# A transposed feed-forward group taken whole: all wide products, then all narrow ones

## The chip, the cores and the metric

The kernel runs on one core of one Trainium2 chip. Time is device time in microseconds (us). The median of three runs before the change is 970.79 us (970.16 to 971.24).

The engines are TensorE (PE in the profile; PEld is its weight load), VectorE (DVE), ScalarE (ACT), GpSimd (POOL) and SyncE (SP), which here issues the transfers. Each works through its own queue in order. [...]

## The reference

Two decoder layers on 256 tokens of width 1024, in float32. Each layer has a feed-forward half step, a token mixer and a second feed-forward half step, each followed by a residual sum and a layer norm. So there are four feed-forward phases, and the change concerns only these:

```
def swiglu(x, w_gate, w_up, w_down):
    return (jax.nn.silu(x @ w_gate) * (x @ w_up)) @ w_down

x = layer_norm(ALPHA * x + 0.5 * swiglu(x, ffn1_gate[l], ffn1_up[l], ffn1_down[l]), ...)
```

The hidden width is 2816, the model width 1024.

## The kernel before

**Numbers.** A float32 matrix is split in two float32r parts: the high part (`xh`, `wh`, `dh`, `hth`) is a cast by ScalarE, the low part (`xl`, `wl`, `dl`, `htl`) a subtraction by VectorE (`halves`, L100 to L102). A product is made of three: high by high, high by low, low by high. `mm3` (L94 to L98) issues them one after the other, each of 512 columns.

**Tiling.** The hidden width is cut in 11 groups of 256 (`GW`). A group has four weight tiles of gate and up together (`gw[g]`, one for every two of the eight slices of 128 of the model width) and two of down (`dw[g]`). `G` makes gate and up of a group and `D(g, hf)` adds the group's down product for one half (128) of the tokens: twelve products, six into each of two banks.

**Turned groups.** Groups 2 to 9 (`turned`, L299) are computed transposed: the weights are the stationary operand (128 columns of the hidden width, a block `i` of two in a group), and the tokens move. Here the three products become two: a *wide* one, the high weights by high and low tokens side by side (512 columns, L314), and a *narrow* one, the low weights by the high tokens (256 columns, L312), which is added to the right half of the same bank. `G(g, n)` of a turned group makes block `n`: two banks, gate and up, and for each of the four weight tiles four wide and then four narrow products (`columns`, L302). Then `gate_turned` (L317) reads the banks: ScalarE copies the right half, VectorE adds the left half (L324, L325), and so for gate and for up; then silu, a product, and the split into `hth` and `htl`. The other groups (0, 1 and 10) have the tokens as the stationary operand; their result is transposed on TensorE by `T` (L396, L399), whose bank is then read by ScalarE and VectorE.

**Banks.** Eight: four called `acc` (`psa`), which hold the down sums, and four called `gu` (`psg`), which `G`, `T` and the transposes of the tokens take in turn, in a ring. Who writes a bank waits until its last content has been read.

**Weights.** They come in one fixed order (`stream`) through five staging tiles (`raw`), and are split into a ring of eight (`w`), of eight (`x`) or of six (`d`, down). `advance` loads on as far as rings are free; a tile's place is free after its last use (`used`, L145). ScalarE and VectorE take the splits and the read-outs from one queue each, in an order fixed when the program is built; `gate_turned`, `gate` and `T` ask for a higher priority than program order (`AHEAD`), weight splits for a lower one (`BEHIND`).

**Order on TensorE.** It is written out by hand in `run` (L431). In the loop over the turned groups, G(g, 0), D(g - 1, 0), G(g, 1), D(g - 1, 1) follow each other. `Later` keeps short pieces of work, such as `T`, that become due after so many ticks; a tick is three products of 512 columns (`mm3`) or as much (L315). `later.wait` issues due work early until a condition holds.

Of the kernel before, what the change touches and what calls it, by code (L numbers as in the profile page):

```python
# [10 lines left out]
F32 = mybir.dt.float32  # L11
# [6 lines left out]
P = 128  # L18
D = 1024
S = 256  # L20
DEPTH = 2
KT = D // P
DFF = 2816
GW = 256
# [50 lines left out]
def trunk(ctx: ExitStack, tc: tile.TileContext, t, out: bass.AP):  # L75
    nc = tc.nc
# [9 lines left out]
    psg = pool("psg", 4, space=PSUM)  # L86
    ctx.enter_context(tc.manual_schedule(engines={mybir.EngineType.PE}))
    later = Later()
# [80 lines left out]
    x, xT = [None, None], [None, None]  # L169
    xt2 = xtp.tile([P, KT, 2, 2, P], F32R, name="xt")  # L170
# [19 lines left out]
    def project(hf, ps, ws):  # L190

        xt = xT[hf]
        for kt in range(KT):
            later.wait(lambda: xt.done > kt)
            wh, wl = ws[kt // 2].parts
            cs = slice((kt % 2) * 512, (kt % 2) * 512 + 512)
            mm3(ps, xt.h[:, kt, :], xt.l[:, kt, :], wh[:, cs], wl[:, cs], kt == 0, kt == KT - 1)
            if kt % 2:
                ws[kt // 2].used()
# [66 lines left out]
    class FFN:  # L266
# [14 lines left out]
                for n in {0: [], 1: [0, 1], 2: [], NG - 1: [NG - 2, NG - 1]}.get(g, [g - 1]):  # L281
                    self.dw[n] = [Weight(dn[2 * n + i], "d", ND) for i in range(2)]

        def G(self, g, n):

            if self.turned(g):
                ps = [psg.tile([P, 2 * S], F32, name="gu") for _ in range(2)]
                for kq, w in enumerate(self.gw[g]):
                    later.wait(lambda: min(xT[0].done, xT[1].done) > 2 * kq + 1)
                    self.columns(kq, n, ps, w)  # L290
                    w.used()
                self.gate_turned(g, n, ps)
                return
            hf = n
            ps = psg.tile([P, 2 * GW], F32, name="gu")
            project(hf, ps, self.gw[g])
            self.gate(g, hf, ps)

        def turned(self, g):  # L299
            return 1 < g < NG - 1  # L300

        def columns(self, kq, i, ps, w):  # L302


            parts = [(kt, part) for kt in range(2) for part in range(2)]
            for lo in range(2):
                for kt, part in parts:
                    c = kt * 512 + part * GW + i * P
                    x = xt2[:, 2 * kq + kt].rearrange("p l h t -> p (l h t)")
                    first, last = kq + kt == 0, kq == KT // 2 - 1 and kt == 1  # L310
                    if lo:
                        nc.tensor.matmul(ps[part][:, S:2 * S], w.parts[1][:, c:c + P], x[:, 0:S], start=False, stop=last)  # L312
                    else:
                        nc.tensor.matmul(ps[part], w.parts[0][:, c:c + P], x, start=first, stop=False)  # L314
                later.tick()  # L315

        def gate_turned(self, g, i, ps):  # L317
            gate = scope[0].tile([P, S], F32, name="sil", bufs=2)
# [87 lines left out]
        def D(self, g, hf):  # L406
            if self.turned(g):
                ht = [[p[:, place[hf], :] for p in self.ht[g, i]] for i in range(2)]
            else:
                later.wait(lambda: (g, hf) in self.ht)  # L410
                ht = [[p[:, i, :] for p in self.ht[g, hf]] for i in range(2)]
            if g == 0:
                self.accs[hf] = [psa.tile([P, 512], F32, name="acc") for _ in range(2)]
            if g == 4 and hf == 0:
                self.gb = load_gb(*self.ln)
                if self.first:
                    load_consts()
                    for n in range(2):
                        load_x(n)
            dw = [w.parts for w in self.dw[g]]  # L420
            for c in range(2):
                cs = slice(c * 512, c * 512 + 512)
                for i in range(2):
                    mm3(self.accs[hf][c], ht[i][0], ht[i][1], dw[i][0][:, cs], dw[i][1][:, cs],
                        g == 0 and i == 0, g == NG - 1 and i == 1)
            for w in self.dw[g]:
                w.used()
            if g == NG - 1:
                layer_norm(hf, self.accs[hf], 0.5 / ALPHA, self.gb, self.slots[hf], self.last)

        def run(self):  # L431
            G, D = self.G, self.D
            if self.first:
                self.start()
                D(0, 0)
                D(0, 1)
                G(2, 0)
                D(1, 0)
                D(1, 1)
                G(2, 1)  # L440
            else:
                G(0, 0)
                G(1, 0)
                D(0, 0)
                G(0, 1)
                D(1, 0)
                G(1, 1)
                D(0, 1)
                G(2, 0)
                D(1, 1)  # L450
                G(2, 1)
            for g in range(3, NG - 1):
                G(g, 0)
                D(g - 1, 0)
                G(g, 1)
                if g < NG - 2:
                    D(g - 1, 1)
            G(NG - 1, 0)
            D(NG - 2, 0)
            D(NG - 1, 0)  # L460
            G(NG - 1, 1)
            if self.mixer_next:
                tc.keep_in_program_order(nc.scalar.preload_act_table_set("natural_log_exp_and_others"))
            if self.first:
                with tc.high_priority(offset=-BEHIND):
                    lower_bounds()
            for g in range(NG - 3, NG):
                D(g, 1)


    def lower_bounds():

        pr = rawp.tile([P, 2, 512], F32, name="raw")
        for i in range(2):
            late_dma(pr[:, i, :], t["lb"][i:i + 1, :].to_broadcast([P, 512]))
        p0, p1 = pr[:, 0, :], pr[:, 1, :]
        m, r = la, lm
        nc.vector.tensor_tensor(m, p0, p1, ALU.max)
        for p in (p0, p1):
            nc.vector.tensor_tensor(p, p, m, ALU.subtract)  # L480
            tc.keep_in_program_order(nc.scalar.activation(p, p, AF.Exp))
        nc.vector.tensor_tensor(m, p0, p1, ALU.add)
        for c in range(4):
            cs = slice(c * P, (c + 1) * P)
            nc.vector.reciprocal(r[:, cs], m[:, cs])
        for p in (p0, p1):
            nc.vector.tensor_tensor(p, p, r, ALU.mult)
        nc.vector.tensor_tensor(p1, p0, p1, ALU.add)
        nc.vector.tensor_tensor(p1, p1, p0, ALU.subtract)
        nc.vector.tensor_scalar(p0, p1, -1.0, 1.0, ALU.mult, ALU.add)  # L490
        for dst, v in ((m, p1), (r, p0)):
            nc.vector.tensor_scalar_max(dst, v, TINY)
            nc.scalar.activation(dst, dst, AF.Ln)
            nc.vector.tensor_scalar(v, v, 0.0, NEG, ALU.is_le, ALU.mult)
            nc.vector.tensor_tensor(dst, dst, v, ALU.add)
# [372 lines left out]
```

## Time and profile before

| | before |
|---|---|
| median of three runs | 970.79 us |
| profiled execution | 972.56 us |
| its span | 970.7 us |
| granted TensorE clock | 0.999 |
| busy: PE | 958.2 us (99%), 4814 products |
| busy: DVE | 677.4 us (70%) |
| busy: ACT | 525.6 us (54%) |
| DMA | 180.67 MB, mean 186 GB/s |

The span runs from the first to the last instruction of the profiled execution; the profiled execution took 1.86 us more than its span. A row of the page's groups has line, engine, operation, output<-inputs, shape and count, then busy time and mean duration, then the idle time ahead of it and what ended that. In a timeline a row has start, duration, engine, line, operation and count; neighbours of one line are merged, and [..] is the idle time before it and what ended it. Matmuls overlap, so the distance of their starts is their pace, not their duration. Names of tiles that share a buffer can stand for each other (`xh` for `wh`). The three later phases begin near 298, 485 and 776 us.

### The profile page before, as it was taken

What the parts mean: (1) busy time and instruction counts of PE and PEld (TensorE: products, weight loads), DVE (VectorE), ACT (ScalarE), POOL (GpSimd) and SP (SyncE); (2) the same over time, 40 slices, a digit from 0 to 9 for tenths busy, and PEclk for the clock granted to TensorE, in tenths of its full rate; (3) what the DMA queues carried; (4) which work ended last, traced back from release to release, by engine and by line L of the source; (5) the groups of instructions that cost most, each with busy time, mean ns of one, the idle gap of its engine ahead of it and who ended that gap; (6) DMA issues with size and microseconds to landing.
All of it is one profiled execution on the core that took longest, in us unless ns stands there. A gap on an engine that the chain in (4) does not pass through costs nothing.

```text
span 970.7 us, 13157 instructions
## 1 busy us (share of the span) xinstructions
PE 958.2 (99%) x4814; PEld 806.8 (83%) x4814; DVE 677.4 (70%) x1095; ACT 525.6 (54%) x810; POOL 26.2 (3%) x47
## 2 busy tenths in 40 slices
PE   9999999999999999999999999999999999999996
PEld 6888888788888888888788888888888888888885
DVE  5875765799779775665677666647897897665525
ACT  6765655367456664545436555533965466555420
POOL 0000000000010000000000000000001000000000
PEclk9999999999999999999999999999999999999999
DMA  8888654334436876555347755442334378755301
GB/s 283 327 299 301 227 209 161 109 109 132 151 111 229 309 243 217 196 195 173 104 162 251 262 186 208 166 139 97 131 130 168 101 275 286 239 199 208 109 1 44
DMA packets 51473, 180.67 MB, mean 186 GB/s; under 512 B 6096, under 2 KB 6352, under 8 KB 51408
## 3 DMA queue, kind: packets, MB, share of 16 engines
q1 hardware_dynamic: 51408, 179.83, 54.0%
q8 instruction: 38, 0.62, 0.3%
q14 instruction: 27, 0.22, 0.1%
HBM read 178.75 MB, written 1.05 MB: 185 GB/s over the span
## 4 chain that ended last, share of the span: by engine, by line
PE 95%; DMA 2%; DVE 1%; ACT 1%; issue 0%; SPq 0%; DVEq 0%
PE gu L314 23%; PE gu L312 12%; PE acc L97 10%; PE acc L95 10%; PE acc L96 10%; PE gu L97 8%; PE gu L95 8%; PE gu L96 8%; PE acc L650 2%; DMA raw<-in_dn 2%; PE gu L185 1%; PE acc L622 1%; PE acc L623 1%; DMA raw<-in_gu 1%; PE gu L399 1%
## 5 line engine op out<-in xcount | busy, mean ns | idle before, releaser
L102 DVE TENSOR_TENSOR wl<-raw,wh 128x1024 fp32r<-128x1024 f32 (+1 forms) x204 | 243.0, 1202 | 66.5 <-ACT wh L101 59.8
L101 ACT CAST wh<-raw 128x1024 fp32r<-128x1024 f32 (+1 forms) x204 | 210.3, 1035 | 97.1 <-PE gu L314 46.3
L314 PE MATMUL gu<-xt,wh 128*128 128x512 f32 x768 | 208.9, 393 | 0.0
L102 DVE TENSOR_TENSOR dl<-raw,dh 128x1024 fp32r<-128x1024 f32 x88 | 106.7, 1223 | 69.9 <-ACT dh L101 69.5
L314 PEld LDWEIGHTS gu<-xt,wh 128*128 128x128 f32 x768 | 134.6, 189 | 20.6
L95 PE MATMUL acc<-dh,hth 128*128 128x512 f32 x352 | 139.2, 395 | 1.8 <-ACT hth L101 1.8
L97 PE MATMUL acc<-dh,htl 128*128 128x512 f32 x352 | 138.7, 394 | 0.9 <-DVE htl L102 0.8
L96 PE MATMUL acc<-dl,hth 128*128 128x512 f32 x352 | 138.0, 392 | 0.0
L95 PE MATMUL gu<-wh,xt 128*128 128x512 f32 x336 | 135.1, 402 | 0.0
L97 PE MATMUL gu<-wh,xt 128*128 128x512 f32 x336 | 131.3, 391 | 0.0
L312 PEld LDWEIGHTS gu<-xt,wl 128*128 128x128 f32 x768 | 117.7, 189 | 16.0
L96 PE MATMUL gu<-wl,xt 128*128 128x512 f32 x336 | 130.9, 390 | 0.0
L101 ACT CAST dh<-raw 128x1024 fp32r<-128x1024 f32 x88 | 91.8, 1049 | 65.6 <-DMA raw<-in_dn 64.7
L312 PE MATMUL gu<-xt,wl 128*128 128x256 f32 x768 | 122.1, 281 | 0.0
L97 PEld LDWEIGHTS acc<-dh,htl 128*128 128x128 f32 x352 | 66.0, 188 | 16.8 <-DVE htl L102 2.9
L95 PEld LDWEIGHTS acc<-dh,hth 128*128 128x128 f32 x352 | 66.2, 188 | 14.6 <-ACT hth L101 3.2
L96 PEld LDWEIGHTS acc<-dl,hth 128*128 128x128 f32 x352 | 66.2, 188 | 11.9
L97 PEld LDWEIGHTS gu<-wh,xt 128*128 128x128 f32 x336 | 63.1, 188 | 13.6
L96 PEld LDWEIGHTS gu<-wl,xt 128*128 128x128 f32 x336 | 63.3, 188 | 12.1
L95 PEld LDWEIGHTS gu<-wh,xt 128*128 128x128 f32 x336 | 63.2, 188 | 12.0
L314 PE MATMUL gu<-xt,xh 128*128 128x512 f32 x256 | 70.3, 396 | 0.0
L324 ACT COPY sil<-gu 128x256 f32<-128x256 f32 x64 | 23.5, 368 | 68.8 <-PE gu L312 68.8
(156 smaller groups left out, 1049.3 us busy)
## 6 DMA issues: line engine op xcount, KB each, us to landing
raw<-in_gu SPq DMA_DIRECT2D x172, 512.0 KB, 4.5
raw<-in_dn SPq DMA_DIRECT2D x88, 512.0 KB, 4.9
raw<-in_win SPq DMA_DIRECT2D x40, 512.0 KB, 4.3
raw<-in_wout SPq DMA_DIRECT2D x16, 512.0 KB, 4.3
lng<-in_ln_g SPq DMA_DIRECT2D x6, 512.0 KB, 4.8
lnb<-in_ln_b SPq DMA_DIRECT2D x6, 512.0 KB, 5.9
raw<-in_gu SPq DMA_DIRECT2D x8, 256.0 KB, 6.7
raw<-in_cumM SPq DMA_DIRECT2D x2, 512.0 KB, 5.3
```

Of the source, the lines that this page charges most:

```text
L95: nc.tensor.matmul(ps, lh, wh, start=start, stop=False)
L96: nc.tensor.matmul(ps, lh, wl, start=False, stop=False)
L97: nc.tensor.matmul(ps, ll, wh, start=False, stop=stop)
L101: first = nc.scalar.copy(dst_h, src)
L102: return first, nc.vector.tensor_tensor(dst_l, src, dst_h.bitcast(F32), ALU.subtract)
L185: nc.tensor.transpose(pt[:, k - a, :], self.nat[:, k * P:(k + 1) * P], ident)
L312: nc.tensor.matmul(ps[part][:, S:2 * S], w.parts[1][:, c:c + P], x[:, 0:S], start=False, stop=last)
L314: nc.tensor.matmul(ps[part], w.parts[0][:, c:c + P], x, start=first, stop=False)
L324: nc.scalar.copy(dst, p[:, S:2 * S])
L399: nc.tensor.transpose(pt[:, i, :], hn[:, i * P:(i + 1) * P], ident)
L622: nc.tensor.matmul(pe, lh[:, hs], cumM[:, hf, cs], start=True, stop=False)
L650: nc.tensor.matmul(ps[B][0:rows, j, :], E[:, j, s0:s0 + rows], E[:, j, t0:t0 + ps[B].shape[2]], start=True, stop=True)
```

## The change

`G(g, 0)` and `G(g, 1)` of a turned group become one `GT(g)`. It takes all four `gu` banks, issues 32 wide products (per slice of the model width: gate and up of block 0, then of block 1), then the 16 narrow products of block 0, calls `gate_turned` for it, then the 16 of block 1, and `gate_turned` again. A weight tile is marked as used within the last 16 products. Ticks come every 3 x 512 columns. If the group before is not a turned one, `GT` first issues that group's transposes `T`, as far as they are still pending. In `run`, both D of the group before follow GT together (only the first for the last turned group, whose second follows at the end as before).

```diff
@@ -281,38 +281,43 @@
                 for n in {0: [], 1: [0, 1], 2: [], NG - 1: [NG - 2, NG - 1]}.get(g, [g - 1]):
                     self.dw[n] = [Weight(dn[2 * n + i], "d", ND) for i in range(2)]
 
-        def G(self, g, n):
-
-            if self.turned(g):
-                ps = [psg.tile([P, 2 * S], F32, name="gu") for _ in range(2)]
-                for kq, w in enumerate(self.gw[g]):
-                    later.wait(lambda: min(xT[0].done, xT[1].done) > 2 * kq + 1)
-                    self.columns(kq, n, ps, w)
-                    w.used()
-                self.gate_turned(g, n, ps)
-                return
-            hf = n
+        def G(self, g, hf):
             ps = psg.tile([P, 2 * GW], F32, name="gu")
             project(hf, ps, self.gw[g])
             self.gate(g, hf, ps)
 
+        def GT(self, g):
+            later.wait(lambda: self.turned(g - 1) or all((g - 1, hf) in self.ht for hf in range(2)))
+            ps = [[psg.tile([P, 2 * S], F32, name="gu") for _ in range(2)] for _ in range(2)]
+            n = 0
+            for lo in range(2):
+                w = S if lo else 2 * S
+                blocks = [[0], [1]] if lo else [[0, 1]]
+                for block in blocks:
+                    for kt in range(KT):
+                        later.wait(lambda: min(xT[0].done, xT[1].done) > kt)
+                        weight = self.gw[g][kt // 2]
+                        for i in block:
+                            for part in range(2):
+                                c = (kt % 2) * 512 + part * GW + i * P
+                                x = xt2[:, kt].rearrange("p l h t -> p (l h t)")
+                                nc.tensor.matmul(ps[i][part][:, 2 * S - w:], weight.parts[lo][:, c:c + P], x[:, 0:w],
+                                                 start=kt == 0 and not lo, stop=kt == KT - 1 and lo == 1)
+                                n += w
+                                if n >= 3 * 512:
+                                    n -= 3 * 512
+                                    later.tick()
+                        if kt % 2 and block == [1]:
+                            weight.uses = 1
+                            weight.used()
+                    if lo:
+                        self.gate_turned(g, block[0], ps[block[0]])
+
         def turned(self, g):
             return 1 < g < NG - 1
-
-        def columns(self, kq, i, ps, w):
-            parts = [(kt, part) for kt in range(2) for part in range(2)]
-            for lo in range(2):
-                for kt, part in parts:
-                    c = kt * 512 + part * GW + i * P
-                    x = xt2[:, 2 * kq + kt].rearrange("p l h t -> p (l h t)")
-                    first, last = kq + kt == 0, kq == KT // 2 - 1 and kt == 1
-                    if lo:
-                        nc.tensor.matmul(ps[part][:, S:2 * S], w.parts[1][:, c:c + P], x[:, 0:S], start=False, stop=last)
-                    else:
-                        nc.tensor.matmul(ps[part], w.parts[0][:, c:c + P], x, start=first, stop=False)
-                later.tick()
 
         def gate_turned(self, g, i, ps):
             gate = scope[0].tile([P, S], F32, name="sil", bufs=2)
@@ -429,15 +434,14 @@
                 layer_norm(hf, self.accs[hf], 0.5 / ALPHA, self.gb, self.slots[hf], self.last)
 
         def run(self):
-            G, D = self.G, self.D
+            G, GT, D = self.G, self.GT, self.D
             if self.first:
                 self.start()
                 D(0, 0)
                 D(0, 1)
-                G(2, 0)
+                GT(2)
                 D(1, 0)
                 D(1, 1)
-                G(2, 1)
             else:
                 G(0, 0)
                 G(1, 0)
@@ -446,13 +450,11 @@
                 D(1, 0)
                 G(1, 1)
                 D(0, 1)
-                G(2, 0)
+                GT(2)
                 D(1, 1)
-                G(2, 1)
             for g in range(3, NG - 1):
-                G(g, 0)
+                GT(g)
                 D(g - 1, 0)
-                G(g, 1)
                 if g < NG - 2:
                     D(g - 1, 1)
             G(NG - 1, 0)
```

## The prediction

> **What bounds the kernel now.** I read the page first (span, chain, costliest groups; L102 is the split of a weight's low half on VectorE, 1.2 us each).
>
> ```profile
> span 970.7 us, 13157 instructions
> PE 95%; DMA 2%; DVE 1%; ACT 1%; issue 0%; SPq 0%; DVEq 0%
> L102 DVE TENSOR_TENSOR wl<-raw,wh 128x1024 fp32r<-128x1024 f32 (+1 forms) x204 | 243.0, 1202 | 66.5 <-ACT wh L101 59.8
> L314 PE MATMUL gu<-xt,wh 128*128 128x512 f32 x768 | 208.9, 393 | 0.0
> ```
>
> TensorE sets the end: it is the chain for 95% of the span. The change removes no product, so it can gain in two ways only: the same products following each other closer, or a wait of TensorE going away. The durations (393 ns for a wide product) overlap and say nothing about pace; pace is read from starts. So next the timeline of TensorE at the end of a feed-forward phase (start, us, line, count): the 16 wide and 16 narrow products of G(9,1), then G(10,0) and D(9,0), which are wide throughout.
>
> ```profile
> 161.82 1.07 PE L314 MATMUL gu<-xt,wh 128*128 128x512 f32 x4
> 162.73 0.64 PE L312 MATMUL gu<-xt,wl 128*128 128x256 f32 x4
> 163.21 1.09 PE L314 MATMUL gu<-xt,wh 128*128 128x512 f32 x4
> 164.14 0.64 PE L312 MATMUL gu<-xt,wl 128*128 128x256 f32 x4
> 164.61 1.09 PE L314 MATMUL gu<-xt,xh 128*128 128x512 f32 x4
> 165.54 0.64 PE L312 MATMUL gu<-xt,xl 128*128 128x256 f32 x4
> 166.02 1.10 PE L314 MATMUL gu<-xt,xh 128*128 128x512 f32 x4
> 166.95 0.63 PE L312 MATMUL gu<-xt,xl 128*128 128x256 f32 x4
> 167.42 0.40 PE L95 MATMUL gu<-wh,xt 128*128 128x512 f32 x1
> ...
> 169.26 0.39 PE L97 MATMUL gu<-wh,xt 128*128 128x512 f32 x1
> ...
> 172.89 0.39 PE L95 MATMUL acc<-dh,hth 128*128 128x512 f32 x1
> ```
>
> G takes 167.42 - 161.82 = 5.60 us. Its four narrow runs take 0.48, 0.47, 0.48 and 0.47, so 0.119 per product. Its wide runs take 0.91 for the first, which follows wide products, and 0.93 for the others, which follow narrow ones. After the last narrow run the first eight wide products take 1.84 (0.230 each), the next sixteen 3.63 (0.2269 each). So wide products have a settled pace of 0.2269, and a switch from narrow to wide costs some of the following products a few ns each, until they settle.
>
> Is that price one of the switch, or a debt that each narrow product leaves? The mixer shows wide products behind a run of small ones (128 columns) that begins at 740.06:
>
> ```profile
> 740.06 0.60 PE L704 MATMUL gu<-ident,y 128*128 128x128 f32 x4
> ...
> 742.51 0.39 PE L96 MATMUL gu<-wl,xt 128*128 128x512 f32 x1
> ...
> 744.12 0.39 PE L97 MATMUL gu<-wh,xt 128*128 128x512 f32 x1
> ...
> 745.48 0.39 PE L97 MATMUL gu<-wh,xt 128*128 128x512 f32 x1
> ```
>
> Seven products in 1.61 (0.230 each), then six in 1.36 (0.2267 each): more than 2 us of small products leave what 0.47 us of narrow ones leave. It looks like a price of the switch. But the small ones are of another kind, so this is an argument by likeness.
>
> **The change part by part.**
>
> *Fewer switches, all 32 turned groups.* Before, a group has eight narrow-to-wide switches; after, one. Its 32 wide products start behind wide ones (D), so they run settled: 32 x 0.2269 = 7.26. For 32 narrow ones in a row no row exists. In the quads they take 0.1175 to 0.120; I take 0.1195, near the later ones of a run: 3.82. Together 11.08 against 2 x 5.60 = 11.20: 0.12 per group, 3.8 us over 32. For the bounds of the unknown narrow pace the nearest row is that of the wide ones, whose settled pace is 0.0056 from that in the quads (0.93/4 = 0.2325): taken with either sign for the narrow ones, it moves the sum by 32 x 32 x 0.0056 = 5.7 us both ways.
>
> *The two down products side by side.* The first D behind narrow products pays the switch; the second, now behind the first, does not.
>
> ```profile
> 67.11:69.88 2.77, 2.77 (x14) 2.25 (x13) 2.33 (x6) 1.91 (x4) 0.00 (x0) 1.00 0.77 280
> 172.89:175.62 2.73, 2.73 (x13) 2.21 (x12) 1.33 (x3) 0.39 (x1) 0.00 (x0) 1.00 0.00 0
> 349.11:352.42 3.31, 3.05 (x15) 2.18 (x14) 3.22 (x5) 1.93 (x5) 0.00 (x0) 1.00 0.57 194
> 536.57:539.70 3.13, 3.05 (x14) 2.18 (x13) 2.72 (x4) 1.66 (x4) 0.00 (x0) 1.00 0.58 219
> 827.44:831.25 3.81, 3.25 (x15) 2.10 (x13) 3.34 (x5) 2.54 (x6) 0.00 (x0) 1.00 0.37 130
> ```
>
> These are stretches by engine (length first): a D behind narrow products 2.77, behind wide ones 2.73. Six pairs in each of four phases (groups 3 to 8) become neighbours: 24 x 0.04 = 1.0 us.
>
> *A stall that loses its place.* The last three rows are D(2,0) of the second, third and fourth phase: 0.54, 0.36 and 1.04 over 2.77, 1.9 us together. It waits for the low half of group 2's second block, made on VectorE behind the split of down weights that are just landing:
>
> ```profile
> PE acc L97 <- DVE htl L102: 0.8, 2, 0.6
> ```
>
> Only G(3,0) (5.6 us) lies between that block and D(2,0). After the change D(1,1) and all of group 3 do, 2.75 + 11.1 us; the weights are then 5.5 us less urgent too. I count 1.9 as gone.
>
> *A wait that is new: the transpose T(1,1) ahead of GT(2).* GT takes all four banks of `psg`. In the later three phases T(1,1), so far issued after eight products of G(2,0), has to be issued before GT(2), and its bank is the last of the four in the ring: GT's fourth product waits until ScalarE and VectorE have both read it. Everything on TensorE's queue stands behind that product. The rows: start of G(2,0), of T(1,1) (L399), and the VectorE operation that frees the bank, in three phases.
>
> ```profile
> 329.28 1.09 PE L314 MATMUL gu<-xt,xh 128*128 128x512 f32 x4
> 330.69 0.38 PE L399 MATMUL gu<-ident,hn 128*128 128x128 f32 x2
> 330.82 0.71 PE L314 MATMUL gu<-xt,xh 128*128 128x512 f32 x2
> 333.58 0.42 DVE L102 TENSOR_TENSOR htl<-gu,hth 128x256 fp32r<-128x256 f32 x1
> 516.75 1.09 PE L314 MATMUL gu<-xt,xh 128*128 128x512 f32 x4
> 518.15 0.38 PE L399 MATMUL gu<-ident,hn 128*128 128x128 f32 x2
> 518.98 0.42 DVE L102 TENSOR_TENSOR htl<-gu,hth 128x256 fp32r<-128x256 f32 x1
> 807.62 1.09 PE L314 MATMUL gu<-xt,xh 128*128 128x512 f32 x4
> 809.02 0.38 PE L399 MATMUL gu<-ident,hn 128*128 128x128 f32 x2
> 810.21 0.42 DVE L102 TENSOR_TENSOR htl<-gu,hth 128x256 fp32r<-128x256 f32 x1
> ```
>
> The bank comes free 334.00 - 330.69 = 3.31, 1.25 and 1.61 after T's start. GT's fourth product is due 0.13 + 3 x 0.23 = 0.82 after it. With the same latencies the stalls are 2.49, 0.43 and 0.79: 3.7 us, the value I take. Low bound: the shortest three times, 1.3. High bound: VectorE does it no earlier than now while T starts where G(2,0) did: 3.90 + 1.83 + 2.19 = 7.9. In the first phase T(1,1) comes due two ticks, six wide products, before GT(2), 1.4 us: nothing.
>
> *Four banks held at once.* Each next group writes the third and fourth bank 0.46 and 0.69 us after its start; both must have been read by then. Cover is the work between: two D (5.5 us) in steady state, one D (2.75) between GT(2) and GT(3) in three phases. VectorE's last read of a G's banks, for the slowest one (D after it starts at 827.44), a steady one (358.01) and the common quick one (D from 366.38):
>
> ```profile
> 830.86 0.41 DVE L325 TENSOR_TENSOR hn<-gu,hn 128x256 f32<-128x256 f32 x1
> 358.01 0.39 PE L95 MATMUL acc<-dh,hth 128*128 128x512 f32 x1
> 360.30 0.41 DVE L325 TENSOR_TENSOR hn<-gu,hn 128x256 f32<-128x256 f32 x1
> 366.38 0.40 PE L95 MATMUL acc<-dh,hth 128*128 128x512 f32 x1
> 367.25 0.41 DVE L325 TENSOR_TENSOR hn<-gu,hn 128x256 f32<-128x256 f32 x1
> ```
>
> That is 3.83, 2.70 and 1.28 us. Against 5.5 + 0.69 even the slowest is covered: nothing in steady state. Against 2.75 + 0.69 = 3.44 the slowest lacks 0.39: 0 to 1.2 us over three phases, I take 0.4.
> [...]
>
> *At no cost:* weights are freed later inside a group, low halves all within its last 16 narrow products, some 1.9 us. Each ring holds the weights of groups far ahead, and the D pair with the next group hides the splits; without that cover it would be one split, 1.2 us, per weight. Ticks per group stay at sixteen.
>
> **Sum.** -4.8 - 1.9 + 3.7 + 0.4 = -2.6 us. The profiled execution took 972.56 with a span of 970.7, so 970.0 and 968.1; the median shown, 970.79, is 1.77 below that execution, and the forecast on its scale is **968.2**.
>
> **The rivals.**
>
> *The narrow products owe it.* If the extra time behind narrow products is a debt of each of them, 32 in a row slow down or pass it on, and the 4.8 is not gained: 970.8 - 1.9 + 3.7 + 0.4 = 973.0. For it: no long narrow run exists in the trace. Against: a far longer run of small products leaves no more than four narrow ones.
>
> *T is quick.* Now issued earlier, its two readers stand ahead of the weight splits: 1.3 instead of 3.7, no second bank wait: 965.4. For it: ScalarE and VectorE serve it within 1.25 us once of three.
>
> *T stays late.* 7.9 instead of 3.7: 972.4. For it: in-order queues in which splits wait for transfers.
>
> *The banks are not free in steady state* (slower). Place: the start of GT(g+1) behind D(g-1,1), 24 times. It decides from a read-out of 6.2 us after the group's end. Both blocks' read-outs now come 1.9 us apart, and four low-half splits of some 1.2 us become ready at that moment: slowest read-out 3.83 plus three splits would be 7.4, 1.2 over, 29 us: 997. Against: steady read-outs take 1.28 to 2.70, and they are issued at a higher priority than the splits.
>
> **How the numbers follow.** Forecast 0.45 (own range 966 to 970), debt 0.15, T quick 0.18, T late 0.15, banks 0.07. Less than 0.2% (1.9 us) can't be told from no change here. Faster: most of the forecast (0.36) and T quick (0.18), 0.54. Within: the rest of the forecast, T late, a third of the debt, 0.28. Slower: 0.18. The range reaches from somewhat below T quick to the debt: 963.8 to 972.9, most of what the narrow pace leaves open (962.5 to 973.9).
>
> **What would show it.** Narrow starts 0.1195 apart through a group and wide ones 0.227 show the first step right; narrow ones above 0.123 show it wrong. D(2,0) at 2.77 or less in all phases shows the second. A gap at the fourth product of GT(2), released by the VectorE split of the transposed block, is the new wait; its length against 2.49, 0.43 and 0.79 tests the third. Any gap at the third or fourth product of GT(4) to GT(9) would make the prediction wrong.

## The result and the profile after

| | before | after |
|---|---|---|
| median, runs side by side | 970.53 us (969.71 to 971.73, 10 runs) | 976.06 us (972.89 to 978.77, 10 runs) |
| ratio to before, 95% interval | | 1.0057 (1.0043 to 1.0070) |
| span of the profiled execution | 970.7 us | 974.7 us |
| granted clock in it | 0.999 | 0.995 |

The change makes the kernel slower by 0.57%, and its runs scatter over 5.9 us where those before scatter over 2.0. The forecast, 968.2 within 963.8 to 972.9, was wrong in sign and missed the range.

The page after:

```profile
span 974.7 us, 13133 instructions
PE 957.0 (98%) x4814; PEld 808.3 (83%) x4814; DVE 661.6 (68%) x1095; ACT 520.1 (53%) x810; POOL 26.2 (3%) x47
L307 PE MATMUL gu<-xt,xh 128*128 128x512 f32 x256 | 64.9, 405 | 5.0 <-DVE htl L102 5.0
```

The products are the same 4814, and TensorE is busy a little less long than before (958.2), yet the span is longer: on balance time is lost between products, not in them. One group of products has an idle time that no turned group had before, 5.0 us, ended by VectorE's `htl`. The list of TensorE's waits says how often:

```profile
PE gu L307 <- DVE htl L102: 5.0, 3, 2.2
PE acc L95 <- ACT hth L101: 1.8, 4, 0.5
PE gu L376 <- DVE zero L373: 1.1, 1, 1.1
PE acc L95 <- ACT wh L101: 1.0, 1, 1.0
PE gu L404 <- DVE hn L341: 0.5, 2, 0.3
```

Three times, 2.2 us at most. The timeline of TensorE shows where (start, duration, line, count; in brackets the idle time and what ended it): GT(2) of the second phase, of the third and of the fourth, each time ahead of its fourth product.

```profile
329.89 0.44 PE L404 MATMUL gu<-ident,hn 128*128 128x128 f32 x2 [0.32 <-DVE hn L341]
330.08 0.95 PE L307 MATMUL gu<-xt,xh 128*128 128x512 f32 x3
...
333.22 0.97 PE L307 MATMUL gu<-xt,xh 128*128 128x512 f32 x3 [2.19 <-DVE htl L102]
...
522.48 0.74 PE L307 MATMUL gu<-xt,xh 128*128 128x512 f32 x2 [1.38 <-DVE htl L102]
...
814.31 0.96 PE L307 MATMUL gu<-xt,xh 128*128 128x512 f32 x3 [1.47 <-DVE htl L102]
```

VectorE's own timeline beside the first of them:

```profile
330.35 2.49 DVE L102 TENSOR_TENSOR wl<-raw,wh 128x1024 fp32r<-128x1024 f32 x2 [0.51 <-ACT wh L101]
332.75 0.42 DVE L102 TENSOR_TENSOR htl<-gu,hth 128x256 fp32r<-128x256 f32 x1
```

Two weight splits stand ahead of the read-out that frees T's bank. Each of them starts only when ScalarE has cast the same weights, and both casts (at 329.27 and 330.53) had waited for a transfer to land. TensorE stands still meanwhile. What comes then is in the stretches of the same phase (length, busy time, granted clock, share of DMA, GB/s): GT(2), D(1,1), GT(3), the pair of D, GT(4), and a piece of GT(2) behind the wait.

```profile
330.08:345.40 15.32, 13.13 (x66) 0.89 0.61 228
345.40:348.15 2.75, 2.75 (x14) 1.00 0.57 185
348.15:359.24 11.09, 11.09 (x65) 1.00 0.72 214
359.24:364.71 5.47, 5.47 (x26) 1.00 0.62 180
364.71:375.88 11.17, 11.17 (x65) 1.00 0.64 219
334.37:337.78 3.41, 3.41 (x10) 0.50 0.55 219
```

GT(2) takes 15.32 instead of the 11.18 that it takes in the first phase: 2.36 us of waiting over the pace, 0.2 at its first and fourth product, and a stretch of 3.41 us in which the clock is granted at half, which costs some 1.7, half of its length. The other groups take 11.09 to 11.22 and no product in them waits.

**Where the 4.0 us of the two profiles are.** Cut at the start of group 2 and at the start of G(10,0), the profiles give:

| stretch | before | after | difference |
|---|---|---|---|
| start | 36.47 | 35.98 | -0.49 |
| turned groups, phase 1 | 130.95 | 130.11 | -0.84 |
| phase 2 | 129.04 | 131.52 | +2.48 |
| phase 3 | 128.88 | 129.11 | +0.23 |
| phase 4 | 129.54 | 129.21 | -0.33 |
| between and behind them | 415.82 | 418.73 | +2.91 |

The GT(2) of the later three phases are 4.14, 1.72 and 1.83 over the 11.18, 7.69 us together. Without them the four phases gain 6.15: 1.94 from D(2,0), 0.42 from T's products that moved ahead of the stretch, and 3.8 from the pace. Of the +2.91 between, 0.42 is those products of T, 0.72 is T's wait for its input ahead of GT(2); nearly all of the rest, some 1.6, are waits of 0.2 to 0.6 at T(10,0), T(0,0) and D(0,0).

### The profile page after: what moved, and what is told of

Its sections match the earlier page's. It is cut to its first block, busy times and chain, and to the rows that moved or that the text cites. A ratio compares the mean times of both kernels' runs of the same rounds, so it can differ in the third digit from the quotient of the medians.

```text
span 974.7 us, 13133 instructions
## 1 busy us (share of the span) xinstructions
PE 957.0 (98%) x4814; PEld 808.3 (83%) x4814; DVE 661.6 (68%) x1095; ACT 520.1 (53%) x810; POOL 26.2 (3%) x47
## 4 chain that ended last, share of the span: by engine, by line
PE 62%; DVE 4%; DMA 3%; ACT 1%; issue 1%; DVEq 0%; SPq 0%; ACTq 0%
PE gu L307 27%; PE acc L95 6%; PE acc L97 6%; PE acc L96 6%; PE gu L97 4%; PE gu L95 4%; PE gu L96 4%; DMA raw<-in_gu 2%; DVE wl L102 2%; DMA raw<-in_dn 1%; PE acc L652 1%; DVE dl L102 1%; PE gu L185 1%; ACT wh L101 0%; PE acc L624 0%
## 5 line engine op out<-in xcount | busy, mean ns | idle before, releaser
L307 PE MATMUL gu<-xt,wh 128*128 128x512 f32 x768 | 179.7, 390 | 0.0
L307 PEld LDWEIGHTS gu<-xt,wh 128*128 128x128 f32 x768 | 144.4, 188 | 30.4
L307 PE MATMUL gu<-xt,wl 128*128 128x256 f32 x768 | 99.7, 283 | 0.0
L307 PEld LDWEIGHTS gu<-xt,wl 128*128 128x128 f32 x768 | 96.9, 191 | 2.0
L330 DVE TENSOR_TENSOR sil<-gu,sil 128x256 f32<-128x256 f32 x64 | 27.0, 422 | 86.1 <-ACT sil L329 86.1
L307 PE MATMUL gu<-xt,xh 128*128 128x512 f32 x256 | 64.9, 405 | 5.0 <-DVE htl L102 5.0
```

Source lines behind the costliest of these rows:

```text
L307: nc.tensor.matmul(ps[i][part][:, 2 * S - w:], weight.parts[lo][:, c:c + P], x[:, 0:w], start=kt == 0 and not lo, stop=kt == KT - 1 and lo ...
L330: nc.vector.tensor_tensor(dst, p[:, 0:S], dst, ALU.add)
```

## The experiments

Two theories. **W**: the loss is the wait at GT(2)'s fourth product and the half clock behind it; the gain in the groups is there. **R**: taking a group whole costs something everywhere (four banks held, weights freed late).

### Groups 2 and 3 as before, the others whole

`G2` is the turned `G` of the kernel before, one block of a group.

```diff
-                GT(2)
+                G2(2, 0)
                 D(1, 1)
-            for g in range(3, NG - 1):
+                G2(2, 1)
+                G2(3, 0)
+                D(2, 0)
+                G2(3, 1)
+                D(2, 1)
+            for g in range(3 if self.first else 4, NG - 1):
```

> Groups 2 and 3 of the three later phases are taken as before (block by block, with the down products between, T(1,1) inside G(2,0)); all other turned groups stay whole as in the change. Theory W (the loss sits at the fourth product of GT(2), which waits for the bank of T(1,1), and in the half clock that follows the wait; the gain of fewer switches is there in all groups): no wait at GT(2), the gain of 8 + 3 x 6 whole groups at 0.12 us remains, 3.0, and the wait of D(2,0) comes back: about 967.5 us, clock as before. Rival R (whole groups cost something everywhere: four banks held, weights freed late): still above the kernel before, 973 or more.

969.68 us (967.24 to 973.02, 11 runs), ratio 0.9988 (0.9977 to 0.9998); the profiled execution has a span of 967.0. The whole groups are worth keeping, which speaks against R, but the median is 2 us above what W expected. No wait at group 2's products is left in the list, and the wait of D(2,0), which was expected to come back, is 0, 0.3 and 0 us in the three phases; in the profile T(0,0) and D(0,0) of the second phase wait 0.6 and 0.5 us, as in the change, for reasons that come from transfers (below), and its runs scatter as widely as the change's.

### Wide products block by block

```diff
-                blocks = [[0], [1]] if lo else [[0, 1]]
+                blocks = [[0], [1]]
 ...
-                        if kt % 2 and block == [1]:
+                        if lo and kt % 2 and block == [1]:
```

> The change, but the 32 wide products are issued block by block: 16 of block 0, then 16 of block 1, then the narrow ones as in the change. The last two banks are needed 3.6 us later, by which time the bank of T(1,1) has been read (3.3 us after T at the latest in the profile after). Theory W: the wait of 5.6 us in three phases and the half clock go, the rest of the change stays: 970.5 - 3.7 - 1.9 + 0.7 = 965.6, between 965 and 967. Rival R: 973 to 976, as the change.

967.31 us (967.08 to 969.28, 5 runs), ratio 0.9970 (0.9958 to 0.9982): 8.7 us below the change by another order of two loops, and faster than the kernel before. Stretches of GT(2) and GT(3) in the second phase:

```profile
330.19:341.52 11.33, 11.33 (x66) 1.00 0.67 243
344.27:355.36 11.09, 11.09 (x65) 1.00 0.72 244
```

GT(2) is back at 11.33 at a full clock, although T is still issued directly ahead of it, two splits (at 329.93 and 332.54) still run before its read-out, and all four banks are still taken at once. Only the time at which T's bank is first needed has moved, by 14 wide products. That settles W against R. All five runs lie above the 965 to 967 expected. In the profile, of the slowest of them (969.28), the four phases together gain 5.7 us; 1.2 are lost between them, and 1.2 at the start of the kernel, where TensorE waits for 1.69 us and the clock then falls to half for 3.41. What the other four runs lose is not known.

### Products that fill the wait

```diff
+                                if g == 2 and not self.first and (lo, kt, i, part) == (0, 0, 1, 0):
+                                    idle = ident.bitcast(mybir.dt.bfloat16)
+                                    for _ in range(14):
+                                        nc.tensor.matmul(ps[1][0][:, 0:256], idle[:, 0:P], idle, start=True, stop=True)
```

> The change, with 14 products of 256 columns (bf16, some 1.5 to 3 us in all) issued ahead of the third product of GT(2) in the three later phases, into a bank that the third product then overwrites; nothing else changes. TensorE is busy through most of the wait. Theory W with the half clock as a result of the idle wait: the wait for the bank stays (it ends when VectorE is done), but the granted clock stays at 1.00 behind it: 2 to 4 us below the change, 972 to 974, with little scatter. If the half clock has another cause: as the change, 976, with its scatter of 6 us.

974.56 us (972.30 to 977.06, 6 runs), ratio 1.0039 (1.0026 to 1.0052). GT(2) of the three phases:

```profile
329.78:343.13 13.35, 13.13 (x81) 1.00 0.67 240
517.91:530.77 12.86, 12.86 (x82) 1.00 0.66 248
809.93:823.25 13.32, 13.09 (x80) 1.00 0.69 250
```

The stretches are still 1.7 to 2.2 us too long, since the bank is freed no sooner; but the clock stays at 1.00 in all three. Over all runs the median granted clock is 0.998, where the change has 0.9955. So the half clock follows idleness. The median falls by 1.5 us, less than the 2 to 4 expected, the intervals of the two ratios overlap, and the scatter stays at 4.8 us, which I had expected to go.

### The switches alone

```diff
-                for kq, w in enumerate(self.gw[g]):
-                    later.wait(lambda: min(xT[0].done, xT[1].done) > 2 * kq + 1)
-                    self.columns(kq, n, ps, w)
-                    w.used()
+                for lo in range(2):
+                    for kq, w in enumerate(self.gw[g]):
+                        later.wait(lambda: min(xT[0].done, xT[1].done) > 2 * kq + 1)
+                        self.columns(kq, n, ps, w, lo)
+                        if lo:
+                            w.used()
 ...
```

This is an edit of the kernel before; `columns` issues the wide products when `lo` is 0 and the narrow ones when it is 1.

> The kernel before with one change: G(g, n) issues its 16 wide products, then its 16 narrow ones, in its two banks; the order of G and D is that before. Two switches per block pair from narrow to wide instead of eight, no whole group, no early T. If the gain is that of the switches (0.12 us per group for seven of them): six sevenths of 3.7, so 3.2 us below before, 967.3, with the waits of D(2,0) still there. If the gain belongs to the whole group (one run of 32, or the two down products side by side): 970.5, as before.

967.83 us (967.34 to 969.49, 6 runs), ratio 0.9972 (0.9961 to 0.9983). In its profile the turned phases take 130.33, 127.85, 127.85 and 127.85. Without the D(2,0) waits (0.54, 0.36, 1.04) that is 0.62 to 0.67 less than before in each, 2.6 us in all (3.2 expected): switches have a price, and two runs per block save two thirds of the 3.8 us that whole groups with neighbouring D save. The D(2,0) waits are gone too, although the order of TensorE's steps is that of before: on ScalarE the high half of group 2's second block (345.93) now stands ahead of the cast of the down weights (348.20), where it stood behind it (348.95 behind 347.99). So queue order alone removes that wait, without the distance that I had argued with. The landing of the weights decides as well: with groups 2 and 3 as before, the cast still stands ahead of the high half, but in the fourth phase it starts 2.2 us ahead of D(2,0) (823.21 and 825.42) instead of 0.6 (826.83 and 827.44), and D(2,0) does not wait.

### More cover for T

```diff
                 G(0, 1)
+                G(1, 1)
                 D(1, 0)
-                G(1, 1)
                 D(0, 1)
                 GT(2)
```

> The change with one step of the three later phases moved: D(1,0) stands behind G(1,1) instead of ahead of it. T(1,1) then comes due by its ticks inside D(0,1), six products (1.4 us) ahead of GT(2), and G(1,1)'s own result has 2.7 us more. Theory W: the waits of T for its input (0.48 and 0.24 us in the profile after) go, the wait at GT(2)'s fourth product shrinks from 2.4, 1.6 and 1.6 to some 1.0, 0.2 and 0.2, so no idle stretch is long enough for the half clock: about 976.1 - 0.7 - 4.2 - 2 = 969. If the waits come from whole groups as such: no change, 976.

969.36 us (967.69 to 970.98, 11 runs), ratio 0.9983 (0.9974 to 0.9992). The waits:

```profile
PE gu L307 <- DVE htl L102: 1.4, 2, 0.8
```

From 5.0 in three to 1.4 in two, and no T waits for its input. The change's whole loss is undone by 1.4 us more between T and GT(2) and as much more between G(1,1) and T. With the block-by-block order as well:

> Wide products block by block (as in the run of that name) and D(1,0) behind G(1,1). The only waits left there, T for its input (0.24 and 0.21 us in the profile of the blockwise kernel), go: 967.3 - 0.5 = 966.8. If the new place of D(1,0) lacks its own input in time: 967.5 to 969.

968.03 us (967.19 to 968.82, 5 runs), ratio 0.9968 (0.9955 to 0.9980): no wait at GT(2) is left in the profile, and nothing is gained over the block order alone. The expected 0.5 us is not there; the time lies in the 967.5 to 969 expected if D(1,0) had to wait for its own input, but the profile shows no such wait.

### T's read-out by priority, and by ScalarE alone

```diff
-            with tc.high_priority(offset=AHEAD):
+            with tc.high_priority(offset=1000):
                 halves(hth, htl, pt)
```

> The change with the priority of T's two read-outs raised, so that the order of VectorE and ScalarE puts them ahead of the weight splits that come due at the same time; the order of TensorE is that of the change. If the wait at GT(2) is the two splits that stand ahead of the read-out on VectorE: the wait shrinks to at least 0.4 us and at most one split, 1.2 us, in each of three phases, the half clock goes: 976.1 - 3 - 2 = 971 or less. If VectorE's order does not matter (the input or ScalarE is late): 975 to 977.

976.49 us (974.55 to 977.99, 5 runs), ratio 1.0053 (1.0040 to 1.0065). This one answers nothing: the order on VectorE stayed as it was, two splits at 329.70 and then the read-out at 332.04. So I took the bank away from VectorE:

```diff
             with tc.high_priority(offset=AHEAD):
-                halves(hth, htl, pt)
+                back = hn.rearrange("p (k t) -> p k t", k=2)
+                nc.scalar.copy(back, pt)
+                halves(hth, htl, back)
```

> The change, but T's bank is read by ScalarE alone: it copies the transposed block back into the tile that T read, and the high part (ScalarE) and the low part (VectorE) are made from that copy. TensorE's order and VectorE's order are not touched; ScalarE has one copy more per T, 0.37 us. Theory W, with VectorE's queue (two splits ahead of the low part) as what holds the bank: the bank is free when ScalarE's first read is done, in the profile after 1.1, 0 and 0.3 us behind the due time of GT(2)'s fourth product instead of 2.4, 1.6 and 1.6; the half clock goes: 976.1 - 4.2 - 2 = 970, at most 971.5. If the bank is not what GT(2) waits for: 976 as the change.

972.91 us (969.44 to 977.70, 12 runs), ratio 1.0026 (1.0011 to 1.0041). Its list of waits:

```profile
PE acc L95 <- ACT hth L101: 3.6, 4, 0.9
PE gu L307 <- ACT hn L409: 1.4, 2, 1.0
```

The wait at GT(2) has a new releaser, ScalarE's copy, and is 1.4 instead of 5.0: VectorE's queue did hold the bank. (The profile is of one of the faster of twelve runs, 970.55; they scatter over 8.3 us.) What I left out is the first row: T(10,0) has nothing to cover it, D(10,0) waits for its `hth`, and the additional copy makes that wait 0.44 us longer in each of four phases (1.8 to 3.6 us). That explains 1.8 of the 2.9 us above the expected 970; the rest stays open. The same edit on the block-by-block order:

> Wide products block by block, and T's bank freed by ScalarE alone. There the bank is no longer waited for, so theory W expects nothing from the second edit: 967.3, within 967 to 968. If T's read-out order costs something there too, below 966.5.

970.05 us (969.44 to 971.71, 11 runs), ratio 0.9991 (0.9983 to 1.0000): 2.7 us above the block order without it. The expected 967.3 missed the same copy: in its profile too the four waits of D(10,0) come to 3.6 us, which is 1.8 of the 2.7.

### The change twice more

> The changed kernel once more, for a second profiled execution: its executions lie between 972.9 and 978.8. Theory W: the waits at GT(2) and at the start of a phase differ from execution to execution, since ScalarE's and VectorE's queues there stand behind splits that wait for transfers to land, and the half clock follows only the longest waits: the whole groups and the mixers take the same to 0.1 us in both profiles, and the difference of the two spans is found in those waits and in the half clock. Rival: the scatter is spread over the groups.

> As the run before: a third profiled execution of the changed kernel, with the same expectation of both theories.

978.45 and 977.05 us, spans 976.7 and 975.2. First the waits at GT(2), then the stretches with the clock, of the one:

```profile
332.66 0.79 PE L307 MATMUL gu<-xt,xh 128*128 128x512 f32 x1 [3.47 <-DVE htl L102]
...
522.47 0.73 PE L307 MATMUL gu<-xt,xh 128*128 128x512 f32 x2 [1.01 <-DVE htl L102]
...
814.74 0.51 PE L307 MATMUL gu<-xt,xh 128*128 128x512 f32 x1 [2.31 <-DVE htl L102]
```

```profile
331.33:338.16 6.83, 5.50 (x13) 0.50 0.57 202
816.03:819.44 3.41, 3.41 (x10) 0.50 0.55 197
```

and of the other, the stretches first:

```profile
333.02:336.44 3.42, 3.42 (x10) 0.50 0.68 267
814.30:817.72 3.42, 3.42 (x10) 0.50 0.94 381
332.08 1.31 PE L307 MATMUL gu<-xt,xh 128*128 128x512 f32 x4 [2.64 <-DVE htl L102]
...
521.26 0.96 PE L307 MATMUL gu<-xt,xh 128*128 128x512 f32 x3 [1.28 <-DVE htl L102]
...
813.27 0.96 PE L307 MATMUL gu<-xt,xh 128*128 128x512 f32 x3 [1.77 <-DVE htl L102]
```

Every other whole group takes the same 11.09, 11.17 or 11.22 us in all three profiles, to 0.01. The three GT(2) are 7.7, 11.9 and 9.9 us over: 5.6, 7.3 and 6.2 of waiting over the pace, and 1.7, 4.5 and 3.4 of half clock (half of the busy time spent in it); what is left is mostly the first product behind T and the first behind the wait, which take some 0.1 us more each. So the scatter of the change is not in the groups: it sits in these places, as W expects, and in part outside the phases. The spans are 4.0, 6.0 and 4.5 us over that of the kernel before, and the 2.4 us that the first profile loses elsewhere are 0.0 and 0.6 in the other two.

## Why the prediction was wrong

**Fewer switches and neighbouring D, forecast -4.8: -3.8 measured.** The mechanism held. Narrow products follow each other at 0.1194 on average (0.1195 taken), and the pair of D takes 5.47 (forecast 5.50). Mis-sized is the group: 11.08 forecast, 11.09 in four of seven steady groups, 11.17 or 11.22 in three, 11.13 on average. The three are those with two of their four weight tiles in the ring `x`. There wide products follow each other at 0.233, not at the 0.227 taken for all (below). The rival that narrow products owe the time is false.

**D(2,0), forecast -1.9: -1.9 measured.** All three take 2.75. The reason given was incomplete: the kernel with two runs per block loses the same wait by queue order alone, and in the change too the high half (349.07) stands ahead of the cast of the down weights (351.95).

**Four banks held at once, forecast +0.4: 0.** No product of GT(3) or of a later group waits in any profile. The cover argued from the rows, two D or one, sufficed; the rival with a price in every group is false.

**T(1,1) ahead of GT(2), forecast +3.7: +5.6, 7.3 and 6.2 in three profiles.** This is the first step that failed. The place, the bank, the releaser and the row to look for were right; the size was not. I took the latencies before the change between T and its read-out, 3.31, 1.25 and 1.61 us. T now comes 1.4 us earlier in the order, and VectorE runs two splits ahead of the read-out in all three phases, so in the first profile the bank came free 3.28, 2.40 and 2.55 us after T. The three waits are 2.36, 1.55 and 1.64 over the pace, where 2.49, 0.43 and 0.79 were forecast: the third and the fourth phase were mis-sized. All three profiles lie between the forecast and the upper bound, 7.9. T also waits for its own input (0.48 and 0.24 us in the first profile), which I had not costed: G(1,1)'s result is ready only just in time.

**Not in the forecast at all: the half clock.** This is the second step that failed: I priced a wait at its own length. Where TensorE stood idle at GT(2) for 1.77 us or more, the clock was granted at half for 3.41 or 6.83 us behind it, and the products then took 0.427 instead of 0.227. That adds 1.7, 4.5 and 3.4 us in the three profiles. With these terms the sum for the first profile is -3.8 - 1.9 + 5.6 + 1.7 and +2.4 for the rest, 4.0 us, the difference of the spans. For the other two it is -3.8 - 1.9 + 7.3 + 4.5, 6.0 but for rounding, and -3.8 - 1.9 + 6.2 + 3.4 + 0.6, 4.5. The half clock alone does not put the time outside the range: the kernel with the filler, whose profile has none during the work, takes 974.56, still over the 972.9 and over the case "T stays late" (972.4).

**Open.** Waits of 0.2 to 0.6 us at the first T and D of a phase (T(10,0), T(0,0), D(0,0)), some 1.6 us in the profile after, occur in some profiles and not in others, of whole-group kernels mostly. They stand behind casts that wait for transfers to land (2.1 us of idle ScalarE in front of the one at 303.45), but why these kernels meet them more often than the kernel before was not tried. Some of the scatter of the kernels with groups 2 and 3 as before, with the filler and with ScalarE's copy is not explained by the clock, which their runs show at 0.995 to 0.999. Why weights in the ring `x` make wide products slower is also open.

## What to carry to other kernels

A reordering that saves nanoseconds on every product can be undone at the few places where the stages meet: ask of each bank that is taken earlier who still has to read it, and what stands ahead of that reader in its queue; use the upper bound when transfers feed that queue. Order the products so that the bank freed last is written last: the same 64 products in another order of loops turned 976.1 us into 967.3. And a TensorE wait near 2 us can cost more than its length, since the half clock may come on top (3.42 us of it behind a wait of 1.77).

## What the runs showed of the hardware

**The clock fell to half behind waits near 2 us and longer, mostly for 3.41 us.** In four profiles of kernels with the whole wait (the change three times, and the kernel with the raised priority), waits at GT(2) of 1.77, 2.19, 2.31, 2.64 and 3.47 us were followed by the half clock (0.50), and waits of 1.01 to 1.74 us (seven) were not. Half clock lasted 3.41 or 3.42 us four times and 6.83 once, when it began while TensorE still waited. A filler of 14 small products in the wait kept the clock at 1.00.

The length of the idle time alone does not decide. At the start of the block-by-block kernel waits of 1.69 and 0.23 us were followed by the half clock, where the wait of 1.74 us with the raised priority was not. Behind the last product the clock stayed at 1.00 for another 2.20 us in the first profile of the change (967.05 to 969.25) and for another 5.34 us in the kernel before (963.09 to 968.43), and only then fell to half. What decides was not shown.

**Wide products are slower where their weights lie in the ring `x`.** The ring has two tiles (`NX`, L38), not eight. Group 4 of the second phase, its first two weight tiles in `w`, the others in `x`:

```profile
364.71 3.80 PE L307 MATMUL gu<-xt,wh 128*128 128x512 f32 x16
368.35 3.90 PE L307 MATMUL gu<-xt,xh 128*128 128x512 f32 x16
372.08 1.11 PE L307 MATMUL gu<-xt,wl 128*128 128x256 f32 x8
```

From start to start the 16 products take 3.64 us and 3.73. Over the groups that follow D, wide products take 0.2271 on average with weights in `w` and 0.2331 in `x`, in all three profiles of the change. In the kernel before, with runs of four, they took 0.2313 and 0.2338: longer runs gain 4 ns per product in `w` and hardly any in `x`. Groups 3, 5, 6 and 8 have no tile in `x` and take 11.09; groups 4, 7 and 9 have two and take 11.17 to 11.22.
